# Hybrid SSD and attention layer on one core: weights times values in float32r high and low parts, head by head, row maxima a head ahead, one ring for the projection weights

## The chip, the cores and the metric

The kernel runs on one core of a Trainium2 chip. The metric is the device time of one execution in microseconds. The core's engines are TensorE (PE in the profile; PEld is its weight loading), VectorE (DVE), ScalarE (ACT), GpSimd (POOL) and SyncE (SP, which issues DMAs). Each runs its own queue of instructions in order.

## The reference

One layer is computed for 2048 new frames of one stream (the prompt) and for 16 frames of each of 8 streams (the sample), all in float32. An input projection is split between a state-space group (SSD) and an attention group of 8 heads of 64; both outputs go through one output projection; a gated feed-forward network with a short convolution follows (width 2816). The part that the change is about is the prompt's attention:

```python
def fox_block(q, k, v, fq, fk, q_pos, k_pos):
    s = jnp.einsum('bqhd,bkhd->bhqk', q, k).astype(jnp.float32) * FOX_SCALE
    s = s + (jnp.swapaxes(fq, 1, 2)[:, :, :, None] - jnp.swapaxes(fk, 1, 2)[:, :, None, :])
    s = jnp.where((k_pos[None, :] <= q_pos[:, None])[None, None], s, -jnp.inf)
    p = jax.nn.softmax(s, axis=-1)
    return jnp.einsum('bhqk,bkhd->bqhd', p.astype(v.dtype), v)
```

## The kernel before, in words

The prompt goes in four parts of 512 tokens (`p` = 0 to 3). For each, `a_head` norms and transposes the rows, the first step of `a_body` projects values, gates, queries and keys, and its second step projects the SSD inputs. Projections, the output projection and the feed-forward network multiply in float32r: both operands are split into a high and a low part (`split`: one engine copies the high part in float32r, another subtracts it to get the low part), and three matmuls are added up (high by high, high by low, low by high). Attention scores are made so too, with two matmuls (lines 576 and 577, or 635 and 636), as the parts are stacked on the 128 rows. The weights times values alone are plain float32 (line 621).

Projection weights come in two shapes. `proj_tm` keeps 128 tokens still and streams 256 or 272 weight columns; its split weights lie in `tmw`, one buffer for all eight row blocks. `proj_cm` keeps 128 weight columns still and streams the tokens; its split weights lie in `cmw`, two buffers, which also take the first input rows.

Attention for one part has two passes over a head's key blocks of 512 keys. `s_phase` makes scores with queries on the partitions, takes the row maximum of each block (line 580), the exponential with its sum (line 581), and, when the head is done, the final maximum and the reciprocal of the sum. These go through `st_d` in DRAM: the maximum comes back as two more rows of the query tile `q12`, the reciprocal into `rdb`. `t_phase` makes the scores again, with keys on the partitions and the maximum already subtracted, takes the exponential (line 640) and multiplies with the values (line 621) into the accumulator `pv`. It works on a pair of heads: for each step of 128 keys both heads' scores, then the weights times values of two steps before, each head on its own 64 columns of TensorE and its own half of `pv`. Line 649 scales by `rdb`. In part `p` there are 4(p+1) steps; the four of the diagonal block have 512, 384, 256 and 128 queries, the others 512.

`attention` runs `t_phase` of a pair with `s_phase` of the next pair strewn in, two steps to one, and with the steps of the SSD chunks (`ssd_chunk`) as side work. The order written in the program is a priority: a planner with its own costs decides the order on every engine, so that projections, output projection and attention mix. All DMAs but the weights' are issued from SP's queue; `dW` issues on ScalarE's.

Of the kernel before, what the change touches and what calls it, by code (L numbers as in the profile page):

```python
# [36 lines left out]
# windows of tokens: (first, end, with the sample's tokens behind them)  # L37
# [14 lines left out]
QB = 5  # L52
PB = 6
# [11 lines left out]
def hybrid_step(ctx: ExitStack, tc: tile.TileContext, i: dict, o: dict):  # L65
# [6 lines left out]
    # per head: queries (high; low) and (high; 1, 1, max high, max low), keys (high; high) and (low; F high, F low, 1, 1)  # L72
# [10 lines left out]
    st_d = dram.tile([H, 4, 3, 512], F32, name="st_d")  # L83
    sf_d = dram.tile([2, NB, H, PAST], F32, name="sf_d")
# [37 lines left out]
    # =================================================================== input projection  # L122
# [28 lines left out]
    def a_head(p, prev):  # L151
        res = []
        first = p == 0
        for e, w in enumerate(part_windows(p)):
# [12 lines left out]
            for c0, n, col, xsrc in groups:  # L167
                N = n * P
                pr = tpt()
                if first:  # L170
                    xa = at([P, 2, KT, P], "cmw", 2).rearrange("p c k d -> p c (k d)")
                    for c in range(n):
                        nc.scalar.dma_start(xa[:, c], i["xr"][c0 + c])
# [35 lines left out]
    def gates(p, dtf):  # L209
# [12 lines left out]
        # log(1 + u) = 2 atanh(u / (2 + u))  # L222
# [35 lines left out]
        # rows of the cumulated decays  # L258
# [9 lines left out]
        # rows of the negated cumulated log forget gates  # L268
# [15 lines left out]
        # the sample: decays of the states, cumulated log forget gates of its cached and new rows  # L284
# [39 lines left out]
    def a_body(p):  # L324
        """Two steps: queries, keys, values and gates; then the SSD inputs."""
        wins = wins_of[p]

        def proj_tm(src, n, use):
            wm = at([P, 2, KT, 272], "tmw", 1, F32R)
            for e in range(2):  # L330
                raw = at([P, 4, 272], "craw", 2)
                dW(raw[:, :, :n], src[:, 4 * e:4 * e + 4])
                split(raw[:, :, :n], wm[:, 0, 4 * e:4 * e + 4, :n], wm[:, 1, 4 * e:4 * e + 4, :n], S, G)
            for w, wt in wins:
                for c in win_tiles(w):
                    ps = mmt()
                    a = PAD1 + (c * P if c != SMP else w[1]) - w[0]
                    for k in range(KT):
                        T.matmul(ps[:, :n], wt[:, 0, k, a:a + P], wm[:, 0, k, :n], start=k == 0, stop=False)  # L339
                        T.matmul(ps[:, :n], wt[:, 0, k, a:a + P], wm[:, 1, k, :n], start=False, stop=False)  # L340
                        T.matmul(ps[:, :n], wt[:, 1, k, a:a + P], wm[:, 0, k, :n], start=False, stop=k == KT - 1)  # L341
                    use(ps, c)
# [108 lines left out]
    # =================================================================== SSD, one chunk of 128 tokens  # L451
# [94 lines left out]
    # =================================================================== prompt attention  # L546
# [67 lines left out]
    def t_phase(pair, qb, qq, rdb):  # L614
# [4 lines left out]
        def weigh(vr, jj, of, prs, first, last):  # L619
            for e in range(2):  # L620
                m = T.matmul(pv[e * 64:(e + 1) * 64, of:512], vr[:, jj, e * 64:(e + 1) * 64], prs[e][:, :512 - of],  # L621
                             start=first, stop=last)
                pv_ins.append(m.ins)

        for kb in order:
            kk = [load_k(2 * pair + e, kb) for e in range(2)]
            vr = load_v(pair, kb)
            for jj in range(4):
# [3 lines left out]
                prs = []  # L632
                for e in range(2):
                    ps = pss()
                    T.matmul(ps[:, :W], kk[e][:, 0, js], qq[e][:, 0, of:], start=True, stop=False)  # L635
                    T.matmul(ps[:, :W], kk[e][0:68, 1, js], qq[e][0:68, 1, of:], start=False, stop=kb != qb)  # L636
                    if kb == qb:
                        T.matmul(ps[:, 0:P], maskT, identb, start=False, stop=True)
                    pr = bt_([P, 528], "pr", PB)
                    S.activation(pr[:, :W], ps[:, :W], AF.Exp)  # L640
                    prs.append(pr)
                if len(late) == 2:
                    weigh(*late.pop(0))
                late.append((vr, jj, of, prs, kb == qb and jj == 0, kb == order[-1] and jj == 3))
# [3 lines left out]
        yl = bt_([P, 512], "yl", 2)  # L648
        V.tensor_mul(yl, pv, rdb)
        dS(mix_d[4 * qb:4 * qb + 4, :, 4 + pair, :].rearrange("c p t -> p c t"), yl.rearrange("p (c t) -> p c t", t=P))  # L650

    def attention(p, others):
        """All heads over the queries of part p, with the steps of other work strewn in; two steps of two pairs each."""
        def scores(pair, done):
            for e in range(2):
                yield from s_phase(2 * pair + e, p, done)

        cur = []
        for _ in scores(0, cur):
            pass  # L660
        for pair in range(4):
            if pair % 2 == 0:
                side = (None for g, _ in others[pair // 2] for _ in g)
                total = sum(n for _, n in others[pair // 2])
                units = 2 * 4 * (p + 1)
                k, given = 0, 0
            nxt = []
            ahead = scores(pair + 1, nxt) if pair < 3 else iter(())
            for _ in t_phase(pair, p, [c[0] for c in cur], cur[0][1]):
                next(ahead, None)  # L670
# [5 lines left out]
            for _ in ahead:  # L676
                pass
            cur = nxt
            if pair % 2:
# [4 lines left out]
    # =================================================================== sample attention  # L684
    def sample_attention():
# [6 lines left out]
        # eh[r, (h, t)] = r == h (rows 0..7 for the high parts, 32..39 for the low ones)  # L692
# [10 lines left out]
        # even and odd heads' rows  # L703
# [7 lines left out]
        # queries of a pair of heads (d of both; t of the one, t of the other)  # L711
# [6 lines left out]
        for b in range(NB):  # L718
# [53 lines left out]
            # ys[d, h, t, b]  # L772
# [4 lines left out]
    # =================================================================== output projection  # L777
# [41 lines left out]
    # =================================================================== FFN  # L819
# [3 lines left out]
    def prep(w, early=False):  # L823
        """The normed rows of a window, transposed and split; the rows themselves stay to be added to."""
# [92 lines left out]
    def ffn_part(x):  # L917
# [4 lines left out]
        for f0 in range(0, NFF, GRP):  # L922
# [10 lines left out]
            if f0 == 0 or f0 + GRP >= NFF:  # L933
                # window by window, so that the next window's rows can be made ready behind the first
# [3 lines left out]
                if f0 == 0 and x == 0:  # L938
                    # the rows to add to are not wanted before the first sums
# [23 lines left out]
    # =================================================================== order of the work  # L963
# [223 lines left out]
```

## Time and profile before

| | us |
|---|---|
| median of 3 runs | 3285.99 |
| lowest and highest run | 3285.44, 3288.5 |
| profiled execution, its span from first to last instruction | 3287.8 |
| TensorE busy in it | 3153.2 |
| VectorE, ScalarE, GpSimd busy in it | 1790.8, 1190.8, 835.9 |

The profiled execution has no time other than its span. The input projection, SSD and attention fill the first 1640 us; the feed-forward network, which the change leaves alone, takes the rest.

### The profile page before, as it was taken

How to read it: one execution, taken by the hardware profiler on the slowest of the kernel's cores; microseconds unless marked ns; L12 is line 12 of the kernel's file. 1: busy time of each engine (PE TensorE's matmuls, PEld its weight loads, DVE VectorE, ACT ScalarE, POOL GpSimd, SP SyncE). 2: the span in 40 equal slices, each digit the busy share in tenths (PEclk: the TensorE clock that was granted, in tenths of full speed). 3: DMA queues.
4: the chain of work that ended last, by engine and by line, in shares of the span. 5: the costliest groups of instructions: out<-in, count | busy, mean ns of one | idle time of the engine just before them, and what ended most of it. 6: DMA issues, size and time to landing. Idle time of an engine off the chain costs nothing.

```text
span 3287.8 us, 46925 instructions
## 1 busy us (share of the span) xinstructions
PE 3153.2 (96%) x18032; PEld 2662.5 (81%) x18032; DVE 1790.8 (54%) x3522; ACT 1190.8 (36%) x2378; POOL 835.9 (25%) x483
## 2 busy tenths in 40 slices
PE   5998989999999998999999999999999999999999
PEld 5876777668667775566689999998999999899998
DVE  5355446555554464334345555557555555766666
ACT  2343344445454455333332222224222223422222
POOL 3221221222131223000032232223222223333332
PEclk8989989999999998999999999999999999999999
DMA  4765875667456755555552122214212212322222
GB/s 148 212 192 178 266 207 175 179 187 211 138 174 171 211 152 178 155 157 158 173 172 64 58 65 64 65 55 138 64 53 76 64 52 71 110 78 75 71 73 70
DMA packets 227720, 423.96 MB, mean 129 GB/s; under 512 B 23264, under 2 KB 100072, under 8 KB 227496
## 3 DMA queue, kind: packets, MB, share of 16 engines
q1 hardware_dynamic: 173928, 259.72, 26.4%
q10 hardware_dynamic: 53568, 161.24, 16.1%
q8 instruction: 142, 2.33, 0.3%
q14 instruction: 82, 0.67, 0.1%
HBM read 342.43 MB, written 78.45 MB: 128 GB/s over the span
## 4 chain that ended last, share of the span: by engine, by line
PE 83%; DMA 10%; DVE 3%; SPq 1%; ACT 1%; issue 1%; POOL 0%; ACTq 0%; DVEq 0%; POOLq 0%
PE mm L112 13%; PE mm L113 13%; PE mm L114 13%; PE pv L621 6%; PE dn L901 5%; PE dn L902 5%; PE dn L903 5%; DMA k<-k_d 3%; PE dn L803 2%; PE dn L802 2%; PE dn L801 2%; PE s L635 2%; PE mm L339 2%; PE mm L340 2%; PE mm L341 2%; PE s L636 2%
## 5 line engine op out<-in xcount | busy, mean ns | idle before, releaser
L104 POOL TENSOR_TENSOR wr<-raw,wr 128x1024 fp32r<-128x1024 f32 x198 | 476.0, 2411 | 1038.7 <-ACT wr L101 1030.6
L112 PE MATMUL mm<-nT,wr 128*128 128x386 f32 (+1 forms) x2112 | 696.5, 330 | 1.5 <-ACT wr L101 1.0
L113 PE MATMUL mm<-nT,wr 128*128 128x386 f32 (+1 forms) x2112 | 695.3, 329 | 0.1
L114 PE MATMUL mm<-nT,wr 128*128 128x386 f32 (+1 forms) x2112 | 694.5, 329 | 0.2 <-POOL wr L104 0.2
L879 DVE SCALAR_TENSOR_TENSOR ac<-mm,cw,ac 128x384 f32<-128x384 f32 (+1 forms) x528 | 301.8, 572 | 345.7 <-ACT ac L877 338.0
L877 ACT ACTIVATE ac<-mm,cw 128x384 f32<-128x384 f32 (+1 forms) x264 | 172.5, 653 | 785.0 <-PE mm L114 777.0
L113 PEld LDWEIGHTS mm<-nT,wr 128*128 128x128 f32 x2112 | 399.4, 189 | 6.7 <-DVE nT L104 0.3
L112 PEld LDWEIGHTS mm<-nT,wr 128*128 128x128 f32 x2112 | 397.5, 188 | 8.1 <-ACT wr L101 1.5
L114 PEld LDWEIGHTS mm<-nT,wr 128*128 128x128 f32 x2112 | 398.0, 188 | 6.3 <-POOL wr L104 0.6
L904 DVE TENSOR_TENSOR y<-y,dn 128x512 f32<-128x512 f32 x374 | 255.2, 684 | 267.3 <-PE dn L903 264.6
L112 PE MATMUL mm<-nT,cmw 128*128 128x256 f32 (+2 forms) x1024 | 308.4, 301 | 14.0 <-ACT ev L395 7.9
L113 PE MATMUL mm<-nT,cmw 128*128 128x256 f32 (+2 forms) x1024 | 305.1, 298 | 0.0
L114 PE MATMUL mm<-nT,cmw 128*128 128x256 f32 (+2 forms) x1024 | 304.6, 297 | 0.0
L580 DVE TENSOR_REDUCE nm<-s 128x1 f32<-128x512 f32 (+2 forms) x320 | 189.8, 606 | 201.7 <-PE s L577 109.3
L901 PE MATMUL dn<-wr,ht 128*128 128x512 f32 x748 | 294.4, 394 | 2.8 <-DVE y L904 1.7
L902 PE MATMUL dn<-wr,ht 128*128 128x512 f32 x748 | 292.7, 391 | 0.0
L903 PE MATMUL dn<-wr,ht 128*128 128x512 f32 x748 | 290.1, 391 | 0.0
L101 ACT CAST wr<-raw 128x1024 fp32r<-128x1024 f32 x198 | 203.4, 1043 | 179.7 <-PE dn L903 161.5
L621 PE MATMUL pv<-pr,v 128*64 128x512 f32 (+3 forms) x640 | 265.1, 568 | 0.5 <-ACT pr L640 0.5
L104 POOL TENSOR_TENSOR cmw<-craw,cmw 128x1024 fp32r<-128x1024 f32 x64 | 154.1, 2409 | 433.0 <-ACT cmw L101 391.9
L581 ACT ACTIVATE s<-s,nm 128x512 f32<-128x512 f32 (+2 forms) x320 | 191.1, 598 | 172.9 <-DVE nm L580 158.4
L640 ACT ACTIVATE pr<-s 128x512 f32<-128x512 f32 (+3 forms) x320 | 163.0, 532 | 203.3 <-PE s L636 130.4
(295 smaller groups left out, 5474.2 us busy)
## 6 DMA issues: line engine op xcount, KB each, us to landing
raw<-in_w_up ACTq DMA_DIRECT2D x132, 512.0 KB
k<-k_d SPq DMA_DIRECT2D x160, 256.0 KB
raw<-in_w_down ACTq DMA_DIRECT2D x66, 512.0 KB
craw<-in_w_cm ACTq DMA_DIRECT2D x64, 512.0 KB
k<-k_d SPq DMA_DIRECT2D x160, 136.0 KB
craw<-in_w_tm ACTq DMA_DIRECT2D x24, 512.0 KB
q_d<-qk SPq DMA_DIRECT2D x96, 128.0 KB
k_d<-qk SPq DMA_DIRECT2D x96, 128.0 KB
```

Source lines behind the costliest of these rows:

```text
L101: S.copy(hi, src)
L104: leng.tensor_sub(lo, src, hi.bitcast(F32))
L112: T.matmul(ps[:, :W], whi(k), wt[:, 0, k, :W], start=k == 0, stop=False)
L113: T.matmul(ps[:, :W], whi(k), wt[:, 1, k, :W], start=False, stop=False)
L114: T.matmul(ps[:, :W], wlo(k), wt[:, 0, k, :W], start=False, stop=k == n - 1)
L581: S.activation(ps[:, :W], ps[:, :W], AF.Exp, bias=nm[:, qi, kb:kb + 1], accum_out=dn[:, qi, kb:kb + 1])
L621: m = T.matmul(pv[e * 64:(e + 1) * 64, of:512], vr[:, jj, e * 64:(e + 1) * 64], prs[e][:, :512 - of], start=first, stop=last)
L879: V.scalar_tensor_tensor(ac[:, 0:n], ps[:, j:j + n], cw2[:, ct, j:j + 1], ac[:, 0:n], op0=ALU.mult, op1=ALU.add)
L901: T.matmul(ps, ht[:, 0, ts_], wd[:, 0, cc], start=x == 0, stop=False)
L902: T.matmul(ps, ht[:, 0, ts_], wd[:, 1, cc], start=False, stop=False)
L903: T.matmul(ps, ht[:, 1, ts_], wd[:, 0, cc], start=False, stop=x == len(g) - 1)
L904: V.tensor_add(ys_[c][:, cc], ys_[c][:, cc], ps)
```

## The change

Comments are gone in the new file; else it is this:

- Values are kept a second time: each tile of projected values is split in high and low part (`vs`, one buffer) and written to `v2_d`, 128 columns a head (64 high, 64 low). `load_v` loads them for one head.
- `t_phase` takes one head. After the exponential, VectorE copies the high part of the weights in float32r and GpSimd subtracts it to get the low part (`pp`). Two float32r matmuls per step, high and low part of the weights, each with the 128 columns of high and low values, fill all of `pv`. At the end of a head ScalarE copies one half of `pv`, VectorE adds the other and multiplies by `rdb`.
- `attention` runs `s_phase` four steps (`LEAD`) further ahead, one step of it to one step of `t_phase`.
- `tmw` is gone: `proj_tm` takes two of three buffers of `cmw` (`WA`), one for each half of the row blocks.
- `q12` has 4 buffers instead of 5, `pr` 3 instead of 6. The buffer of norm2_g is moved to another pool.

```diff
-QB = 5
-PB = 6
+QB = 4
+PB = 3
+WA = 3
+LEAD = 4
...
+    v2_d = dram.tile([NTILE - 1, P, H, 2, HD], F32, name="v2_d")
...
-            wm = at([P, 2, KT, 272], "tmw", 1, F32R)
+            wm = []
             for e in range(2):
                 raw = at([P, 4, 272], "craw", 2)
                 dW(raw[:, :, :n], src[:, 4 * e:4 * e + 4])
-                split(raw[:, :, :n], wm[:, 0, 4 * e:4 * e + 4, :n], wm[:, 1, 4 * e:4 * e + 4, :n], S, G)
+                we = at([P, 2, 4, 272], "cmw", WA, F32R)
+                split(raw[:, :, :n], we[:, 0, :, :n], we[:, 1, :, :n], S, G)
+                wm.append(we)
...
                 dS(o["v"][c][:, half * 256:(half + 1) * 256], vt)
+                if c != SMP:
+                    vs = at([P, 4, 2, HD], "vs", 1, F32R)
+                    p4 = ps[:, 0:256].rearrange("p (h d) -> p h d", h=4)
+                    S.copy(vs[:, :, 0], p4)
+                    V.tensor_sub(vs[:, :, 1], p4, vs[:, :, 0].bitcast(F32))
+                    dS(v2_d[c][:, half * 4:half * 4 + 4], vs.bitcast(F32))
...
-            wc = at([P, 2, KT, P], "cmw", 2, F32R)
+            wc = at([P, 2, KT, P], "cmw", WA, F32R)
...
-    def load_v(pair, kb):
-        vr = bt_([P, 4, P], "v", 2)
-        dma(vr, o["v"][4 * kb:4 * kb + 4, :, pair * P:(pair + 1) * P].rearrange("c p d -> p c d"))
+    def load_v(h, kb):
+        vr = bt_([P, 4, P], "v", 2, F32R)
+        dma(vr.bitcast(F32), v2_d[4 * kb:4 * kb + 4, :, h].rearrange("c p a d -> p c (a d)"))
...
-    def t_phase(pair, qb, qq, rdb):
+    def t_phase(h, qb, q12, rdb, yl):
...
-        def weigh(vr, jj, of, prs, first, last):
-            for e in range(2):
-                m = T.matmul(pv[e * 64:(e + 1) * 64, of:512], vr[:, jj, e * 64:(e + 1) * 64], prs[e][:, :512 - of],
-                             start=first, stop=last)
+        def weigh(vr, jj, of, pp, first, last):
+
+            for a in range(2):
+                m = T.matmul(pv[:, of:512], vr[:, jj], pp[:, a, :512 - of], start=first and a == 0, stop=last and a == 1)
...
+                pr = bt_([P, 528], "pr", PB)
+                S.activation(pr[:, :W], ps[:, :W], AF.Exp)
+                pp = bt_([P, 2, 512], "pp", 3, F32R)
+                split(pr[:, :W], pp[:, 0, :W], pp[:, 1, :W], V, G)
+                late.append((vr, jj, of, pp, kb == qb and jj == 0, kb == order[-1] and jj == 3))
                 yield
         for x in late:
             weigh(*x)
-        yl = bt_([P, 512], "yl", 2)
-        V.tensor_mul(yl, pv, rdb)
...
+        e = h % 2
+        rs, ot = slice(e * 64, e * 64 + 64), slice(64 - e * 64, 128 - e * 64)
+        S.copy(yl[rs], pv[ot])
+        V.tensor_add(yl[rs], yl[rs], pv[rs])
+        V.tensor_mul(yl[rs], yl[rs], rdb[rs])
...
+        ahead = scores()
+        for h in range(H):
+            while len(done) <= h:
+                next(ahead, None)
+            if h == 0:
+                for _ in range(LEAD):
+                    next(ahead, None)
...
+            for _ in t_phase(h, p, *done[h], yl):
                 next(ahead, None)
                 k += 1
...
-    g2B = g2.tile([P, D], F32, name="g2B")
+    one = F.enter_context(tc.tile_pool(name="o3", bufs=1, side="right", reuse_waits="tile"))
+    g2B = one.tile([P, D], F32, name="g2B")
     dA(g2B, i["norm2_g"][0:1, :].to_broadcast([P, D]))
```

## Rows read from the trace of the kernel before

**Rows 1.** The page, its first two parts: busy time, share and instructions of TensorE (PE, and PEld for its weight loads), and the span in 40 equal slices of 82.2 us (tenths busy; PEclk is the granted TensorE clock in tenths of full speed).

```profile
PE 3153.2 (96%) x18032; PEld 2662.5 (81%) x18032; DVE 1790.8 (54%) x3522; ACT 1190.8 (36%) x2378; POOL 835.9 (25%) x483
PE   5998989999999998999999999999999999999999
PEclk8989989999999998999999999999999999999999
```

**Rows 2.** Busy time by stretch of the span, all engines. Columns: stretch, its length, then busy us (x instructions) of PE, PEld, DVE, ACT and POOL, granted clock, DMA share, GB/s.

```profile
0.00:390.00 390.00, 326.24 (x2311) 278.61 (x2311) 190.26 (x544) 135.88 (x321) 100.80 (x75) 0.92 0.64 194
390.00:1350.00 960.00, 903.27 (x5561) 668.10 (x5557) 501.45 (x1146) 466.03 (x1118) 222.96 (x128) 0.96 0.62 182
1350.00:1640.00 290.00, 290.00 (x1286) 187.69 (x1285) 111.25 (x210) 106.20 (x239) 10.08 (x18) 1.00 0.51 157
```

**Rows 3.** The same stretches for line 621 alone, the matmuls of weights times values. Columns: stretch, length, PE busy (x records), PEld busy, granted clock, DMA share, GB/s.

```profile
0.00:390.00 390.00, 20.56 (x64) 5.25 (x64) 0.92 0.64 194
390.00:1350.00 960.00, 178.60 (x416) 35.59 (x416) 0.96 0.62 182
1350.00:1640.00 290.00, 65.99 (x162) 13.05 (x160) 1.00 0.51 157
```

**Rows 4.** The timeline of TensorE at two places of the last part: start us, length us, engine, line, operation.

```profile
1477.02 0.39 PE L635 MATMUL s<-q,k 128*128 128x512 f32 x1
1477.02 0.19 PEld L636 LDWEIGHTS s<-q,k 68*128 68x128 f32 x1
1477.25 0.39 PE L636 MATMUL s<-q,k 68*128 68x512 f32 x1
1477.57 1.07 PE L621 MATMUL pv<-pr,v 128*64 128x512 f32 x2
1478.57 0.50 PE L802 MATMUL dn<-wo,mx 128*128 128x512 f32 x1
1478.91 0.39 PE L803 MATMUL dn<-wo,mx 128*128 128x512 f32 x1
...
1499.55 0.39 PE L636 MATMUL s<-q,k 68*128 68x512 f32 x1
1499.87 1.08 PE L621 MATMUL pv<-pr,v 128*64 128x512 f32 x4
1500.88 0.50 PE L801 MATMUL dn<-wo,mx 128*128 128x512 f32 x1
```

**Rows 5.** The first and the last stretch of line 621 in the timeline of TensorE. In between the 640 records of the line stand in 264 stretches with other instructions between them.

```profile
156.87 1.07 PE L621 MATMUL pv<-pr,v 128*64 128x512 f32 x2
...
1621.88 2.79 PE L621 MATMUL pv<-pr,v 128*64 128x512 f32 x10
```

**Rows 6.** Groups of TensorE's instructions by line and shape: count, busy us, mean ns of one, idle time before them and what ended it.

```profile
L621 PE MATMUL pv<-pr,v 128*64 128x512 f32 x448 | 219.3, 636 | 0.5 <-ACT pr L640 0.5
L339 PE MATMUL mm<-tmw,nT 128*128 128x256 f32 x408 | 121.7, 301 | 4.1 <-ACT tmw L101 2.3 <-ACT ev L349 1.8
L636 PE MATMUL s<-q,k 68*128 68x512 f32 x224 | 92.9, 415 | 11.9 <-DMA q<-st_d 9.5 <-DMA k<-k_d 2.3
```

**Rows 7.** Groups on the other engines, same columns: the nearest operations to those that are added.

```profile
L104 POOL TENSOR_TENSOR nT<-qk,nT 128x512 fp32r<-128x512 f32 x1 | 1.3, 1295 | 5.3 <-ACT nT L101 5.3
L104 POOL TENSOR_TENSOR cmw<-craw,cmw 128x1024 fp32r<-128x1024 f32 x64 | 154.1, 2409 | 433.0 <-ACT cmw L101 391.9 <-PE mm L112 11.8 <-DMA xb_d<-cth 7.7
L103 DVE CAST ht<-ac 128x384 fp32r<-128x384 f32 x110 | 39.3, 357 | 2.9
L103 DVE CAST ht<-ac 128x256 fp32r<-128x256 f32 x22 | 6.3, 287 | 0.4
L649 DVE TENSOR_TENSOR yl<-pv,rdb 128x512 f32<-128x512 f32 x16 | 11.0, 689 | 37.5 <-PE pv L621 30.4 <-DMA out_s_ssdT<-yl 5.7 <-DMA k_d<-qk 1.4
L392 DVE SCALAR_TENSOR_TENSOR qk<-mm,qk 128x256 fp32r<-128x256 f32 x64 | 27.0, 423 | 115.8 <-ACT qk L391 94.0 <-DMA k<-k_d 7.9 <-DMA q_d<-qk 5.4
```

**Rows 8.** One VectorE operation by shape (groups by line), and the timeline of POOL and VectorE where two of their operations meet.

```profile
L890 DVE TENSOR_TENSOR ac<-ac 128x384 f32<-128x384 f32 x110 | 173.5, 1577 | 3.7
L890 DVE TENSOR_TENSOR ac<-ac 128x256 f32<-128x256 f32 x22 | 11.3, 514 | 1.2
...
20.91 2.36 POOL L104 TENSOR_TENSOR nT<-qk,nT 128x1024 fp32r<-128x1024 f32 x1
20.95 2.34 DVE L1001 TENSOR_SCALAR abc<-abc 128x8 f32<-128x8 f32 x1
```

**Rows 9.** The timeline of ScalarE in the first 60 us: the last read of the second tile of input rows, the first cast of projection weights, and two copies of value tiles.

```profile
17.10 0.19 ACT L183 ACTIVATION_READ_ACCUMULATOR cmw<-cmw 128x1 f32 x1
17.29 1.08 ACT L101 CAST tmw<-craw 128x1088 fp32r<-128x1088 f32 x1
...
45.37 0.37 ACT L349 COPY ev<-mm 128x256 f32<-128x256 f32 x1 [1.18 <-PE mm L341]
48.43 0.37 ACT L349 COPY ev<-mm 128x256 f32<-128x256 f32 x1 [2.16 <-issue]
```

**Rows 10.** Two pieces of the chain that ended last (start us, us, what: a DMA from issue to landing, of 128 KB), and the load of the values in the list of DMA issues (count, KB each).

```profile
91.30 2.23 DMA q_d<-qk
387.77 7.43 DMA q_d<-qk
...
v<-out_v SPq DMA_DIRECT2D x40, 256.0 KB
```

More of the change, by code (lines that the diff above doesn't have):

```diff
@@ L617, in t_phase @@
         late = []
-        def weigh(vr, jj, of, prs, first, last):
-            for e in range(2):
-                m = T.matmul(pv[e * 64:(e + 1) * 64, of:512], vr[:, jj, e * 64:(e + 1) * 64], prs[e][:, :512 - of],
-                             start=first, stop=last)
+        def weigh(vr, jj, of, pp, first, last):
+            for a in range(2):
+                m = T.matmul(pv[:, of:512], vr[:, jj], pp[:, a, :512 - of], start=first and a == 0, stop=last and a == 1)
                 pv_ins.append(m.ins)
         for kb in order:
-            kk = [load_k(2 * pair + e, kb) for e in range(2)]
-            vr = load_v(pair, kb)
+            kk = load_k(h, kb)
+            vr = load_v(h, kb)
             for jj in range(4):
@@ L631, in t_phase @@
                 js = slice(jj * P, (jj + 1) * P)
[L632 to L641, printed above, removed]
+                ps = pss()
+                T.matmul(ps[:, :W], kk[:, 0, js], q12[:, 0, of:], start=True, stop=False)
+                T.matmul(ps[:, :W], kk[0:68, 1, js], q12[0:68, 1, of:], start=False, stop=kb != qb)
+                if kb == qb:
+                    T.matmul(ps[:, 0:P], maskT, identb, start=False, stop=True)
                 if len(late) == 2:
                     weigh(*late.pop(0))
-                late.append((vr, jj, of, prs, kb == qb and jj == 0, kb == order[-1] and jj == 3))
+                pr = bt_([P, 528], "pr", PB)
[3 more added lines that the diff above has]
+                late.append((vr, jj, of, pp, kb == qb and jj == 0, kb == order[-1] and jj == 3))
                 yield
@@ L647, in t_phase, with scores @@
             weigh(*x)
-        yl = bt_([P, 512], "yl", 2)
-        V.tensor_mul(yl, pv, rdb)
-        dS(mix_d[4 * qb:4 * qb + 4, :, 4 + pair, :].rearrange("c p t -> p c t"), yl.rearrange("p (c t) -> p c t", t=P))
-    def attention(p, others):
[L654 to L665, printed above, removed]
+        e = h % 2
[3 more added lines that the diff above has]
+        V.tensor_mul(yl[rs], yl[rs], rdb[rs])
+        if e:
+            dS(mix_d[4 * qb:4 * qb + 4, :, 4 + h // 2, :].rearrange("c p t -> p c t"), yl.rearrange("p (c t) -> p c t", t=P))
+    def attention(p, others):
+        done = []
+        def scores():
+            for h in range(H):
+                yield from s_phase(h, p, done)
+        ahead = scores()
+        for h in range(H):
+            while len(done) <= h:
[3 more added lines that the diff above has]
+                    next(ahead, None)
+            if h % 4 == 0:
+                side = (None for g, _ in others[h // 4] for _ in g)
+                total = sum(n for _, n in others[h // 4])
+                units = 4 * 4 * (p + 1)
                 k, given = 0, 0
[L667 to L670, printed above, removed]
+            if h % 2 == 0:
+                yl = bt_([P, 512], "yl", 2)
+            for _ in t_phase(h, p, *done[h], yl):
                 next(ahead, None)
@@ L675, in attention @@
                     given += 1
[L676 to L679, printed above, removed]
+            if h % 4 == 3:
                 for _ in side:
@@ L1057, in hybrid_step @@
     tp = F.enter_context(tc.tile_pool(name="t3", bufs=2, reuse_waits="tile"))
-    g2 = F.enter_context(tc.tile_pool(name="g2", bufs=1, reuse_waits="tile"))
     O = ExitStack()
@@ L1065, in hybrid_step @@
     B.close()
-    g2B = g2.tile([P, D], F32, name="g2B")
+    one = F.enter_context(tc.tile_pool(name="o3", bufs=1, side="right", reuse_waits="tile"))
+    g2B = one.tile([P, D], F32, name="g2B")
     dA(g2B, i["norm2_g"][0:1, :].to_broadcast([P, D]))
-    one = F.enter_context(tc.tile_pool(name="o3", bufs=1, side="right", reuse_waits="tile"))
     yp = F.enter_context(tc.tile_pool(name="y3", bufs=YB, side="right", reuse_waits="tile"))
```

9 lines of the change are left out of this document (5 added, 4 removed).

## Prediction

> **What bounds the kernel now.** I read the page first. TensorE is busy for 96% of the span, and its slices show 9 nearly everywhere after the first half of the attention; the digit of the granted clock falls to 8 only in four of the first 16 slices [rows 1]. So time is TensorE's work plus its idle time plus what runs at half clock. The table by stretch splits the first 1640 us, the only ones that the change touches [rows 2]. From 0 to 390 us (part 0, the sample, the first projections) TensorE idles for 64 us of 390 at clock 0.92: chains between engines set the pace. From 390 to 1350 us it idles for 57 of 960, clock 0.96. From 1350 to 1640 us it never idles, at full clock, with VectorE at 111 and GpSimd at 10 us. I call these A, B and C. The same table for line 621 alone shows what the change attacks: 20.6, 178.6 and 66.0 us, 265 in all [rows 3]. 0.2% (6.6 us) is about what a measurement of this kernel can tell from no change; I use it as the bound below.
>
> **Weights times values on TensorE.** 320 head-steps (a head, 128 keys) are made, 224 of them with 512 queries (448 records in [rows 6], two a matmul) and 96 narrower. The timeline shows one float32 head-step at full width: it starts at 1477.57 and the next instruction at 1478.57, 1.00 us; two heads standing side by side take 1.01 together (1499.87 to 1500.88), since they use different columns [rows 4]. But the planner mostly separates them: 264 stretches for 320 head-steps [rows 5]. Around a stretch there is more: line 636 gives way after 0.32 us instead of 0.23, and the first float32r matmul behind gives way after 0.34 instead of 0.23. That is 0.20 us a stretch, of which 0.07 already counts in the busy time (1.07 drawn, 1.00 to the next start). So 265 + 264 x 0.13 = 299 us: A 24, B 199, C 76.
>
> After, a head-step is two float32r matmuls. At 512 columns such a matmul gives way after 0.23 us [rows 4], so 0.47. For the narrow ones the weight load of 0.19 us is the floor [rows 4]: 0.38. A has 8 wide and 24 narrow head-steps, C about 65 and 15, B the other 151 and 57. At the clocks of [rows 2] that is 12.9 / 0.92 = 14 us in A, 92.6 / 0.96 = 96 in B, 36 in C. TensorE is relieved of 10, 103 and 40 us, 153 in all.
>
> **What is added on the other engines.** Each head-step gets a subtraction on GpSimd: 1.30 us at 512 columns, and by the line through that and 2.41 at 1024 [rows 7], 1.02, 0.74 and 0.46 for the narrow ones: 224 x 1.30 + 32 x 2.22 = 362 us, of which B gets 57 x 0.74 + 151 x 1.30 = 238. It also gets a cast on VectorE, nearest the casts of 357 ns at 384 and 287 at 256 [rows 7], so 0.43 at 512 and 0.22 at 128: 81 us in B. At the end of a head come an add and a multiply on VectorE where a pair had one multiply of 0.69 [rows 7]; half the partitions, the same columns, so I take 0.69 each: 2.1 us more a pair, 20 in B. Each of 32 value tiles gets a copy of 0.37 on ScalarE [rows 9] and a subtraction like the 0.42 of line 392 [rows 7], 10 us of VectorE in B.
>
> These two engines don't run freely beside each other. A multiply on VectorE takes 514 ns at 256 columns and 1577 at 384, and a tiny operation that should take a fraction of a us lasts from 20.95 to 23.29 while a GpSimd subtraction runs from 20.91 to 23.27 [rows 8]: VectorE waits until GpSimd is through. The Trainium skill says why ("SBUF — State Buffer", Who interferes with whom): a VectorE copy or cast in its two-port mode, or an operation with two SBUF inputs, and a GpSimd operation lock each other out for a whole instruction; the trace agrees, 2.34 us beside 2.36. By that rule cast and subtraction cannot overlap, so no step would be shorter than 0.43 + 1.30 = 1.73 us, which by itself would bind nowhere here, but would load VectorE as in the second rival.
>
> In B GpSimd goes from 223 to 461 of 960 us, 48%. A cast that starts meanwhile waits half of a 1.30 or 2.41 us operation, weighted 0.92 us, so 0.44 us on average: 92 us for 208 casts (zero if the planner keeps them apart, 270 if each waits for a whole 1.30). VectorE in B: 501 + 81 + 92 + 20 + 10 = 704 us, of 857 if all of TensorE's relief were kept: 82%, against 52% now. Behind a late cast stand the row maxima (line 580) for the next head; for them waits ScalarE's exponential (line 581), and that frees the four score banks that TensorE writes next. Behind a late subtraction stand the splits of projection weights. TensorE has two steps between scores and weights times values, and a step takes 4.6 us in B (960 / 208), so the new chain of exponential, cast and subtraction mostly fits, and TensorE has other matmuls meanwhile. At 82% with strict order, part of the relief becomes idle time: between all and nothing I take half in B, 52 us. In C VectorE goes from 111 to some 180 of 250 us and GpSimd from 10 to 107: room enough, I keep 40 less 3 for the longer end of each head, 37. There the cover is the output projection's matmuls; without them the last heads would wait 1.7 us a step.
>
> In A the 10 us stand against two losses. `vs` has one buffer: a value tile now takes 0.37 + 0.42 and a DMA, 2.23 us at best and 7.43 at worst for half the bytes [rows 10], so 3.0 to 8.2 us, where copies follow each other after 3.06 us now [rows 9]. With nothing else for TensorE to do at the start, eight tiles may lose 0 to 40 us; the first few hide under the copies of rows still being normed, I take 8. The chain of a step is 1.73 us longer in a part with four steps a head: 8 heads, about half of it uncovered, 7 us. A gives back 5 us.
>
> **Edits that cost nothing or little.** The shared weight ring is free at the start: the second tile of input rows is last read at 17.10, the first weight cast starts at 17.29 [rows 9]. Later a half can be split before the previous projection ends; line 339 idles for 4.1 us at 256 columns. Row maxima a head ahead remove waits for the maximum's way through DRAM, 9.5 us before line 636 [rows 6]. Of these 13.6 us I count 8 (0 to 13.6). Key loads keep their number; with one head per step four buffers reach twice as far ahead. Value loads double, 40 to 80 of 256 KB [rows 10], and 32 writes of 256 KB come: 19 MB and 72 issues more on SP's queue, behind which the key loads stand; the DMA share is 0.62 in B and 0.51 in C [rows 2], so I take nothing and put a few us into the range. Fewer `pr` and `q12` buffers match one head at a time: nothing. The norm2_g buffer is loaded later; its cover is the output projection at the seam, and without that it costs one landing, up to 7.43 us.
>
> **Sum.** B 52 + C 37 - A 5 + 8 = 92 us less. The profiled span of 3287.8 becomes 3195.8; the median of the runs stands 1.8 us below the span, so 3194.
>
> **Rivals.** *All is kept* (15%): the planner hides the longer chain entirely, TensorE stays as full as now; 153 and the 13.6 us of idle time go: 3286 - 167 = 3119. For it speaks that TensorE waits for the exponential for only 0.5 us in 448 wide records [rows 6]; against it, that B already idles for 57 us with VectorE at 52%.
>
> *VectorE becomes the bound in B* (17%): if the waits for GpSimd come at a whole operation, 270 instead of 92 us, VectorE reaches 882 of 857 us. B then keeps nothing; with C at 30 and A at -10, 20 us remain: 3266. The long multiply in [rows 8] speaks for it, where a multiply of 384 columns takes three times one of 256 on average; against it, that row maxima read PSUM and need not wait.
>
> *Slower: TensorE's queue waits for the low part* (10%). Its order is fixed by a planner. If that counts on a shorter subtraction than 1.30 us, or on a GpSimd that isn't in a weight split of 2.41, each head-step's second matmul holds up all that stands behind it. It decides from 153 / 320 = 0.48 us a head-step on; at 0.6 us (half of a split's 2.41 us, met half of the time) the loss is 192 - 153 = 39 us: 3325, before any half-clock time. For it: the 0.5 us of idle time before line 621 [rows 6] come from a chain of one engine, and now three stand in a row. Against it: the two steps of slack.
>
> **How the numbers follow.** The forecast gets 58%; its own range, with 20 to 80% of B kept, is 3225 to 3163. 8 in 10 need most of the VectorE rival too and reach almost to full keeping: 3122 to 3275; outside lie the slower rival, and the better half of the full one. Faster by over 0.2%: 58 + 15 + most of 17, 0.87. Within 0.2%: the thin stretch between the VectorE rival and the slower one, 0.03. Slower: 0.10.
>
> **What would show it.** In the profile after: the new line of weights times values with 640 float32r matmuls, starts 0.23 us apart, some 150 us of TensorE; no 1.00 us holes. GpSimd's subtractions about 360 us, casts of 0.43 us alone and up to 1.7 beside a subtraction; VectorE's busy time up by 150 to 300 us. The seam to the feed-forward network at about 1550 instead of 1640 us, most of it won between 390 and 1350. The step on B is wrong if TensorE's idle time there grows by far more or less than 50 us; the forecast is wrong if TensorE waits before the new matmuls for GpSimd by more than 0.3 us a step, or if the start (up to 120 us) is over 20 us later because of the value tiles.

## The result, and the profile after

The changed kernel takes 3242.17 us (median; 3236.41 to 3244.7) where the kernel before took 3285.72 beside it: a ratio of 0.987, with an interval of 0.9855 to 0.9888. That is 44 us less; 92 were forecast. The profiled execution has a span of 3241.4 us. All of the difference lies ahead of the feed-forward network: its first up-projection matmul starts at 1639.2 us instead of 1684.5, and from there on both kernels take 1.60 ms.

The first part of the page after, as in [rows 1]:

```profile
PE 3038.1 (94%) x18032; PEld 2741.7 (85%) x18032; DVE 2049.0 (63%) x3922; ACT 1216.5 (38%) x2442; POOL 1229.2 (38%) x803
PE   5988889799989997999899999999999999999999
PEclk9999989899989998998999999999999999999999
```

The three stretches of [rows 2] for all engines, and then for the new line 635 alone, as line 621 in [rows 3]:

```profile
0.00:390.00 390.00, 322.97 (x2460) 289.38 (x2461) 220.46 (x626) 152.66 (x363) 140.46 (x110) 0.95 0.70 221
390.00:1350.00 960.00, 854.00 (x5598) 746.24 (x5596) 685.10 (x1398) 482.48 (x1152) 488.33 (x346) 0.93 0.65 196
1350.00:1640.00 290.00, 272.80 (x1310) 214.84 (x1310) 178.57 (x313) 114.40 (x260) 105.07 (x98) 0.95 0.53 176
...
0.00:390.00 390.00, 19.20 (x64) 11.80 (x64) 0.95 0.70 221
390.00:1350.00 960.00, 157.94 (x434) 82.16 (x434) 0.93 0.65 196
1350.00:1640.00 290.00, 54.24 (x142) 28.14 (x142) 0.95 0.53 176
```

From 390 to 1350 us TensorE idles for 106 us instead of 57. The last stretch, full and at full clock before, has 17 us of idle time and a granted clock of 0.95, so a tenth of it runs at 1.2 GHz instead of 2.4.

The groups that answer to [rows 6, 7 and 9]:

```profile
L635 PE MATMUL pv<-pp,v 128*128 128x512 f32 x448 | 181.9, 441 | 35.1 <-DVE yl L663 17.4 <-POOL pp L108 13.1 <-DVE pp L107 3.9
L647 PE MATMUL s<-q,k 68*128 68x512 f32 x224 | 93.2, 416 | 5.3 <-DMA k<-k_d 3.2 <-DMA q<-st_d 2.1
L108 POOL TENSOR_TENSOR pp<-pr,pp 128x512 fp32r<-128x512 f32 x224 | 305.0, 1366 | 352.9 <-DVE pp L107 331.8 <-ACT ev L356 6.7 <-DVE mh L108 5.0
L107 DVE CAST pp<-pr 128x512 fp32r<-128x512 f32 x224 | 137.6, 619 | 48.2 <-ACT pr L653 44.1 <-PE pv L635 3.0
L663 DVE TENSOR_TENSOR yl<-yl,pv 64x512 f32<-64x512 f32 x32 | 21.8, 682 | 12.0 <-ACT yl L662 11.6
L664 DVE TENSOR_TENSOR yl<-yl,rdb 64x512 f32<-64x512 f32 x32 | 27.4, 857 | 0.6
L361 ACT CAST vs<-mm 128x256 fp32r<-128x256 f32 x32 | 12.0, 374 | 35.8 <-DMA v_d<-vs 34.8 <-DVE bs L485 1.0
```

Line 635 waits 35.1 us at full width, where line 621 waited 0.5. The timeline at the end of a head in the last part, TensorE first, then GpSimd, then VectorE at the same time:

```profile
1532.17 0.68 PE L635 MATMUL pv<-pp,v 128*128 128x512 f32 x2
1533.71 0.78 PE L635 MATMUL pv<-pp,v 128*128 128x512 f32 x2 [0.85 <-POOL pp L108]
1535.53 0.74 PE L635 MATMUL pv<-pp,v 128*128 128x512 f32 x2 [1.04 <-POOL pp L108]
...
1532.38 1.28 POOL L108 TENSOR_TENSOR pp<-pr,pp 128x512 fp32r<-128x512 f32 x1 [0.36 <-DVE pp L107]
1534.02 2.70 POOL L108 TENSOR_TENSOR pp<-pr,pp 128x512 fp32r<-128x512 f32 x2 [0.37 <-DVE M L600]
...
1532.22 0.68 DVE L593 TENSOR_REDUCE nm<-s 128x1 f32<-128x512 f32 x1
1532.82 1.12 DVE L107 CAST pp<-pr 128x512 fp32r<-128x512 f32 x1
1534.28 1.23 DVE L107 CAST mh<-M 128x4 fp32r<-128x4 f32 x1
1535.54 1.20 DVE L108 TENSOR_TENSOR mh<-M,mh 128x4 fp32r<-128x4 f32 x1
```

TensorE moves at the pace of GpSimd's subtractions here, two of them in 2.70 us. And VectorE's two operations on 128x4 elements last 1.2 us each, nearly as long as a subtraction of 1.35, and end where the two subtractions end.

### The profile page after: what moved, and what is told of

It reads as the page before. It is cut to its first block, busy times and chain, and to the rows that moved or that the text cites. A ratio compares the mean times of both kernels' runs of the same rounds, so it can differ in the third digit from the quotient of the medians.

```text
span 3241.4 us, 48271 instructions
## 1 busy us (share of the span) xinstructions
PE 3038.1 (94%) x18032; PEld 2741.7 (85%) x18032; DVE 2049.0 (63%) x3922; ACT 1216.5 (38%) x2442; POOL 1229.2 (38%) x803
## 4 chain that ended last, share of the span: by engine, by line
PE 70%; DMA 13%; DVE 10%; issue 3%; ACT 2%; POOL 2%; SPq 1%; ACTq 0%; DVEq 0%; POOLq 0%
PE mm L116 13%; PE mm L117 12%; PE mm L118 12%; PE dn L919 5%; PE dn L920 5%; PE dn L921 5%; PE pv L635 2%; DMA sg<-ac_d 2%; DVE pp L107 1%; PE dn L819 1%; PE dn L820 1%; PE dn L821 1%; DMA k<-k_d 1%; PE s L646 1%; PE s L589 1%
## 5 line engine op out<-in xcount | busy, mean ns | idle before, releaser
L108 POOL TENSOR_TENSOR pp<-pr,pp 128x512 fp32r<-128x512 f32 (+1 forms) x320 | 384.9, 1207 | 469.6 <-DVE pp L107 439.5
L108 POOL TENSOR_TENSOR cmw<-craw,cmw 128x1024 fp32r<-128x1024 f32 (+1 forms) x96 | 234.6, 2446 | 256.1 <-ACT cmw L105 237.9
L635 PE MATMUL pv<-pp,v 128*128 128x512 f32 (+3 forms) x640 | 231.4, 405 | 50.0 <-DVE yl L663 17.4
L653 ACT ACTIVATE pr<-s 128x512 f32<-128x512 f32 (+1 forms) x320 | 167.8, 532 | 182.3 <-PE s L647 118.4
```

Of the source, the lines that this page charges most:

```text
L108: leng.tensor_sub(lo, src, hi.bitcast(F32))
L635: m = T.matmul(pv[:, of:512], vr[:, jj], pp[:, a, :512 - of], start=first and a == 0, stop=last and a == 1)
```

## The account that the experiments share

For each kernel the table by stretch is taken from the start to the first up-projection matmul: length, then busy us of PE, PEld, DVE, ACT and POOL, granted clock. Length less PE is TensorE's idle time. In order: before; after; high half alone, two multiplications; before with float32r; after with the copy on ScalarE; high half alone, one multiplication; float32 at full width.

```profile
0.00:1684.50 1684.50, 1564.01 (x9364) 1171.44 (x9365) 825.91 (x1934) 723.20 (x1710) 338.30 (x234) 0.96 0.61 182
0.00:1639.20 1639.20, 1449.29 (x9365) 1250.30 (x9366) 1083.33 (x2334) 748.89 (x1774) 733.06 (x554) 0.94 0.64 198
0.00:1583.60 1583.60, 1419.27 (x9364) 1244.34 (x9365) 856.92 (x2014) 746.09 (x1774) 342.93 (x234) 0.95 0.66 205
0.00:1577.80 1577.80, 1378.85 (x9044) 1199.83 (x9045) 822.47 (x1934) 736.03 (x1750) 339.14 (x233) 0.94 0.63 194
0.00:1611.80 1611.80, 1438.10 (x9365) 1246.03 (x9366) 923.51 (x2013) 894.50 (x2094) 717.26 (x554) 0.95 0.65 202
0.00:1544.20 1544.20, 1363.57 (x9045) 1190.38 (x9045) 853.82 (x2013) 745.88 (x1774) 341.69 (x234) 0.94 0.67 210
0.00:1629.80 1629.80, 1502.74 (x9365) 1233.34 (x9365) 851.36 (x2013) 753.45 (x1774) 340.77 (x234) 0.97 0.65 199
```

Before to after: TensorE's busy time fell by 115 us, and its idle time rose from 120 to 190, so 45 us were won. The profile's granted clock stands at half (1.2 GHz instead of 2.4) for 140 us before and for 198 after. If half of TensorE's busy time in it counts as lost, that is 60 and 77 us, so 17 us of the relief went to the clock.

Two theories stand from here. **The added chain takes it**: cast and subtraction, on two engines that block each other, cost what is missing. **The relief itself is worth less**: TensorE's matmuls cover the other engines' chains, so of what they give up only a part comes off the end. Times below are medians, with the ratio to the kernel before measured beside each.

## Experiments

**High half alone.** ScalarE's exponential goes to the high half, no copy, no subtraction, both multiplications take that half (it counts double; the low part of the weights is left out):

```
-m = T.matmul(pv[:, of:512], vr[:, jj], pp[:, a, :512 - of], ...)
+m = T.matmul(pv[:, of:512], vr[:, jj], pp[:, 0, :512 - of], ...)
...
-pr = bt_([P, 528], "pr", PB)
-S.activation(pr[:, :W], ps[:, :W], AF.Exp)
+S.activation(pp[:, 0, :W], ps[:, :W], AF.Exp)
-split(pr[:, :W], pp[:, 0, :W], pp[:, 1, :W], V, G)
```

> The changed kernel, with ScalarE's exponential written straight into the high half in float32r; VectorE's copy of the high part and GpSimd's subtraction are gone, and TensorE multiplies the high half twice. The low part of the weights is left out of the result; TensorE's work is the same as in the changed kernel. Theory (the engines behind the split weights eat the gain: 198 us of VectorE, 385 us of GpSimd, and TensorE's waits for the two halves, 47.0 us in 60 waits for the low and 36.2 us in 37 for the high): 50 to 80 us come back, 3162 to 3192 us, and TensorE's idle time up to the first up-projection falls from 193 us towards the 127 us of the kernel before. Rival (TensorE's own work was mis-sized and the waits only move to the next late instruction): under 20 us come back, 3222 us or more.

3186.57 us, 0.971 (0.969 to 0.973): 55 us come back, inside the first theory's range. Third row of the account: TensorE is busy for 30 us less (13 of them because 154 us instead of 198 are at half clock) and idle for 26 us less. But it is 93 us below the kernel before, where the prediction's sum without these two operations would give about 150. Both theories are needed.

**The kernel before, in float32r.** Weights and values are rounded, no low parts (left out), one matmul of 128 columns for a head and step (both heads' values go into the same sums, which this kernel does not tell apart):

```
-QB = 5
+QB = 4
...
+v2 = bt_([P, 4, P], "v2", 2, F32R)
+S.copy(v2, vr)
...
-m = T.matmul(pv[e * 64:(e + 1) * 64, of:512], vr[:, jj, e * 64:(e + 1) * 64], prs[e][:, :512 - of], ...)
+m = T.matmul(pv[:, of:512], vr[:, jj], prs[e][:, :512 - of], ...)
...
-pr = bt_([P, 528], "pr", PB)
+pr = bt_([P, 528], "pr", PB, F32R)
```

> The kernel before, pairs of heads as they were, but weights and values rounded to float32r with no low parts (both are left out of the result), one matmul for a head and step with all 128 columns of the pair; ScalarE rounds each of the 40 value tiles (about 0.6 us each, 24 us in all, a guess from its 128x512 copies), and there are 4 query buffers in place of 5. No copy of high parts and no subtraction. The weighing should take about 320 x 0.23 less the narrow ones = 70 us in place of 244. Theory A (all of 0.20 us for each float32 stretch belonged to the change of type): TensorE's work up to the first up-projection falls by 174 + 53 = 227 us, 3059 to 3085 us with the waits unchanged. Theory B (half of that extra stands around any matmul that waits on a semaphore): it falls by about 200 us, 3086 to 3110 us. Theory C (what TensorE gives up turns into waiting for ScalarE and VectorE in the middle stretch): over 3130 us, with TensorE idle over 180 us in place of 127.

3187.55 us, 0.972 (0.969 to 0.975): theory C. TensorE is busy for 185 us less (fourth row), and nothing was added but 40 copies on ScalarE (with one query buffer less); its idle time still rose from 120 to 199 us. Hardly any of it stands before the weighing:

```profile
L623 PE MATMUL pv<-pr,v 128*128 128x512 f32 x224 | 99.6, 459 | 2.6 <-ACT pr L641 2.6
```

It is spread over the waits that were there before: score banks held by ScalarE, key loads, the row maxima's way through DRAM (17.5 instead of 9.5 us).

**The copy of the high part on ScalarE.**

```
-split(pr[:, :W], pp[:, 0, :W], pp[:, 1, :W], V, G)
+split(pr[:, :W], pp[:, 0, :W], pp[:, 1, :W], S, G)
```

> The changed kernel, with the copy of the high part made by ScalarE right behind its exponential instead of by VectorE; nothing else moves. Takes about 198 us from VectorE's 1083 us ahead of the up-projections and adds about 165 us (320 copies at some 0.5 us) to ScalarE's 749. Theory (VectorE's queue holds the high part up, and VectorE and GpSimd hold each other up): 15 to 40 us faster than the changed kernel, 3202 to 3227 us, and the waits on VectorE's copy, 36.2 us, go. Rival (ScalarE becomes the engine that is late, since the next exponential stands behind the copy): 3242 to 3275 us.

3216.16 us, 0.980 (0.977 to 0.983), and on another chip:

> The kernel with the high part copied by ScalarE once more, beside the two built on it and on the same chip: its ratio to the kernel before was 0.980 (0.977 to 0.983), and the kernel with the carried head ends had 0.984 on another chip. If the carried ends are really slower, this one comes out again at 0.979 to 0.982; if chip and run make the difference, at 0.983 or more.

3210.15 us, 0.9775 (0.975 to 0.980). So 26 to 32 us of the 55 are the copy's place: VectorE goes from 1083 to 924 us, ScalarE from 749 to 895 (fifth row), and ScalarE's queue has the room. It is faster than both kernels given, with the same computation.

**The low part on VectorE too** (the same line with `S, V`):

> The changed kernel with the high part copied by ScalarE and the low part subtracted by VectorE; GpSimd has no part in the weights. VectorE then does 320 subtractions at about 0.65 us where the changed kernel has it do 320 copies at 0.62 us, so its total stays at about 1090 us ahead of the up-projections; GpSimd loses 385 us. Theory (it is the length of the chain, most of it GpSimd's 1.37 us for a subtraction, that TensorE waits for): faster than the kernel with only the copy moved (3216 us), 3190 to 3210 us. Rival (VectorE's load is what makes all other work late): 3225 to 3245 us, as the changed kernel.

3233.95 us, 0.9855 (0.984 to 0.987): no different from the changed kernel and slower than with GpSimd's subtraction, although VectorE's takes 777 ns where GpSimd's takes 1335. The shorter chain did not pay for 223 us on VectorE's queue. Between these two kernels VectorE's load mattered more than the chain's length.

**The accumulator freed without VectorE.**

```
-S.copy(yl[rs], pv[ot])
-V.tensor_add(yl[rs], yl[rs], pv[rs])
+y2 = bt_([P, 512], "y2", 1)
+S.copy(y2[rs], pv[ot])
+S.copy(yl[rs], pv[rs])
+V.tensor_add(yl[rs], yl[rs], y2[rs])
```

> The changed kernel, with ScalarE copying both halves of the accumulator out of PSUM, and VectorE adding them from SBUF, so that the one accumulator is free without VectorE. Theory (the single accumulator, emptied 32 times through VectorE's queue, costs the 32.3 us in 14 waits that stand on VectorE's addition): 10 to 25 us faster than the changed kernel, 3217 to 3232 us. Rival (those waits cover others that stand right behind): 3235 to 3245 us.

3241.66 us, 0.987 (0.985 to 0.990): nothing. The wait named in the profile did go, from 17.4 to 2.5 us, and the line's own from 35.1 to 16.0:

```profile
L635 PE MATMUL pv<-pp,v 128*128 128x512 f32 x448 | 178.5, 434 | 16.0 <-POOL pp L108 9.1 <-DVE pp L107 4.1 <-ACT yl L664 2.5
```

TensorE's whole idle time stayed at 189 us; other waits took the place.

**Head ends carried into the next head.** `late` lives on from head to head (emptied only at heads 3 and 7), and the accumulator is emptied behind its last weighing:

```
...
-        for x in late:
-            weigh(*x)
+        if h % 4 == 3:
+            while late:
+                weigh(*late.pop(0))
```

> The kernel with the high part copied by ScalarE, and in it the last two weighings of a head put behind the first score matmuls of the next head instead of straight behind the last exponential, except at every fourth head; the accumulator is emptied there too. In the changed kernel 22.3 us of TensorE's waits, in 21 places, stand between two weighings at a head's end; with the copy on ScalarE 9.7 us in 17 places. Theory (a head's end has nothing to cover the chain, and there are 32 of them where the kernel before had 16): 6 to 15 us faster than with the copy on ScalarE alone (3216 us), 3201 to 3210 us. Rival (the waits come back a few matmuls later, on the one accumulator): 3212 to 3222 us.

3230.90 us, 0.984 (0.982 to 0.985): 0.4 and 0.6% slower than the two measurements of its base, of which the first one's interval still touches it. Waits between two weighings remained (11 us in 14 places, 7 to 10 in the base). A miss for the theory; why it is slower rather than the same stays open.

**No lead.** `LEAD = 0`:

> The changed kernel with LEAD = 0: the score steps of the next head no longer start four steps early, everything else as it is. Theory (the lead is worth the 9.5 us that the kernel before waits in seven places for the row maxima's round trip through DRAM, and no more): 4 to 12 us slower than the changed kernel, 3246 to 3254 us. Rival (the lead costs as much at each part's start as it brings): 3238 to 3246 us.

3270.91 us, 0.997 (0.996 to 0.998): about 30 us slower, outside both theories. What was to be removed is back, larger than before the change:

```profile
L647 PE MATMUL s<-q,k 68*128 68x512 f32 x224 | 95.8, 427 | 28.7 <-DMA q<-st_d 28.5
```

Our reading: head by head, a next head's maxima have half the time to come back from DRAM that a next pair's had. With the four steps of lead the line waits for 5.3 us.

**More lead.** `LEAD = 8`, with the copy on ScalarE:

> The kernel with the high part copied by ScalarE, and the score steps of the next heads eight steps ahead in place of four. Without a lead the changed kernel took 29 us more, 28.6 us of TensorE's waits standing on the row maxima's way through DRAM. Theory (the more lead the fewer waits): 5 to 15 us faster than the same kernel with a lead of four, 3201 to 3211 us by its first comparison, 3216 us. Rival (four steps have done it already): within 5 us of it.

3235.96 us, 0.986 (0.984 to 0.988), 26 us slower than a lead of four on the same chip. Line 647 waits for nothing, but with a lead of four and the copy on ScalarE it waited for only 0.1 us. TensorE's idle time rose from 170 to 203 us, and the waits for the last VectorE operation on a finished head's sums (line 608) from 11 to 45 us. The transposes of finished heads are among them, with eight steps and with four (the copy on ScalarE, second measurement):

```profile
L613 PE MATMUL s<-ident,rd 128*12 128x128 f32 x32 | 9.6, 299 | 21.7 <-DVE rd L608 21.7
...
L613 PE MATMUL s<-ident,rd 128*12 128x128 f32 x32 | 9.3, 290 | 11.6 <-DVE rd L608 10.8 <-DVE rd L611 0.8
```

**Two buffers for the split values** (`"vs", 2`, with the copy on ScalarE):

> The kernel with the high part copied by ScalarE, and two buffers in place of one for the split values on their way to DRAM. In the changed kernel ScalarE waits 34.8 us for that one buffer. Theory (the wait makes the kernel's start late): 3 to 8 us faster than with one buffer. Rival (other waits of TensorE stand behind it at once): within 3 us of it.

3215.50 us, 0.979 (0.976 to 0.982), against 0.9775 with one: the rival. ScalarE's wait for that buffer fell from 40.6 to 1.9 us, and nothing hung on it. Three buffers were meant for the changed kernel itself, but their pool needs 110.8 KB a partition where 110.5 are left, so that kernel was not measured.

**One multiplication.** The high half alone, `for a in range(1)`; the low part of the weights is left out:

> The kernel with the high half alone (no copy, no subtraction), with one multiplication for a step where it has two: 320 matmuls of the weighing are left out, some 74 us of TensorE's time at 147.6 us for 640; every other engine does the same work. The result leaves the low part of the weights out. Theory (TensorE's own time sets the pace): all of it comes off, 3186.6 - 74 = 3110 to 3120 us. Rival (the matmuls of the weighing cover the other engines' chains, so that what TensorE gives up comes back as waits and as time at the half clock): 20 to 60 % of it comes off, 3142 to 3172 us, with TensorE's idle time ahead of the up-projections up by 25 us or more over 166 us.

3151.11 us, 0.959 (0.957 to 0.962). Of the 74 us reckoned only 35 came off, 47%: the rival. The line itself gave 64 us (147.6 to 83.4 from start to start without idle time; the second matmul of a pair is the cheaper one); the other lines took some 9 us more, and 16 us became idle time (sixth row). So 35 us came off for 56 us less of busy TensorE, 64%. This is the fastest kernel of the study, with weights in float32r without their low part.

**The same, in float32.** The exponential is written in float32, and the matmul reads both operands as float32:

```
-m = T.matmul(pv[:, of:512], vr[:, jj], pp[:, 0, :512 - of], ...)
+m = T.matmul(pv[:, of:512], vr[:, jj].bitcast(F32), pp[:, :512 - of], ...)
-pp = bt_([P, 2, 512], "pp", 3, F32R)
-S.activation(pp[:, 0, :W], ps[:, :W], AF.Exp)
+pp = bt_([P, 512], "pp", 3)
+S.activation(pp[:, :W], ps[:, :W], AF.Exp)
```

> The kernel with one multiplication for a step (3151 us), and in it only the type changed: ScalarE writes the exponential in float32, and TensorE multiplies it in float32 with the same 128 columns (the value tiles still come through float32r, and the high half of the weights is now all of the weights). All other engines, the order and the buffers stay. 320 float32 matmuls of 1.00, 0.78, 0.58 and 0.36 us by the kernel before are some 279 us where 83 stood, 196 more. Theory A (the prediction's: each change of type costs 0.20 us beside, and TensorE's time counts in full): 196 + 64 = 260 us more, 3390 to 3420 us. Theory B (the type alone costs next to nothing beside, TensorE's time counts in full): 3335 to 3365 us. Theory C (in this stretch TensorE's time counts about half, as when the second multiplication was left out, 35 of 74 us): 3240 to 3290 us, with TensorE idle for 40 us or more less than the 181 us of the kernel with one multiplication.

3236.45 us, 0.985 (0.983 to 0.987): below every theory's range, with TensorE idle for 54 us less, as theory C had it. The float32 matmul was cheaper than the kernel before had it. A step at full width, the next matmul, and the one after that:

```profile
908.16 1.08 PE L635 MATMUL pv<-pp,v 128*128 128x512 f32 x2
908.67 0.68 PE L346 MATMUL mm<-cmw,nT 128*128 128x256 f32 x1
909.19 0.28 PE L347 MATMUL mm<-cmw,nT 128*128 128x256 f32 x1
```

It gives way after 0.51 us, and the next matmul after 0.52 instead of its usual 0.12: 0.91 us for the step. By the medians of 195 such steps it is 0.46 and 0.40, and nothing ahead, where 64 columns took 1.00, with 0.09 more ahead and 0.11 behind. TensorE's busy time is 139 us above the float32r kernel's, the time 85: 61%.

This run also says how little of the change's gain needs float32r. It has the full width, the order head by head, the lead and the ring, but float32 weights, no cast and no subtraction, and it leaves nothing out. It takes what the changed kernel takes; their intervals overlap. How that gain divides between the width, the order, the lead and the ring was not measured. From here, float32r with two multiplications is worth 50 us (to 3186.57), and cast and subtraction cost 55.

## Why the prediction was only half right

The direction held, and the time lies inside the range of 3122 to 3275, but outside the likeliest case's own, 3163 to 3225.

- **Losses: right as a sum.** The prediction gave 61 us back (51 in B, 3 in C, 15 in A, less 8 for the edits); TensorE's idle time rose by 69. In B the step held: 49 us more [rows 2, and the table after]. The rest is partly luck: by the same tables A idles for 3 us more and C for 17. The threshold of 0.3 us of waiting for GpSimd a step was never near: 16.4 us before line 635 in all, 0.05 a step. Cast and subtraction cost 55 us by the run without them.
- **The step that failed: 153 us of relief for TensorE**, measured 115. Counted from start to start without idle time, the line went from 247 to 162 us: 85, where the prediction had 100 (246 to 146). The other lines got 30 us shorter, where the 0.20 us around each of 264 stretches should have given 53. What the sum had no term for is a change of the clock: with busy time at half clock counted as half, the line went from 237 to 148 and the other lines from 1267 to 1224, 131 us of relief, and the clock took 17 of it. The rest, 22 us, is in the sizes. One that shows: a float32r matmul of line 635 that starts after idle time gives way after 0.34 us, not 0.23 (21 of 21 at full width).
- **The 0.20 us around a float32 stretch was read rightly.** Against matmuls of the same shape elsewhere, those ahead of a stretch took 0.09 us more and those behind it 0.11 (medians of 264; 55 us together). Around line 635 both medians are 0 (9 us together). Ahead of float32 on 128 columns there is nothing either, so the 0.09 is not the type's alone.
- **The same failure by place: the relief of C, kept in full because TensorE never idled there.** For C the prediction kept 37 of 40. By the first matmul of the output projection 52 us were won (1332.6 to 1280.2), close to the 55 for A, B and the edits; at the seam 45. So C won little or nothing: it lost 7 by this count, with some 10 us more of attention's work left in it. From that matmul to the seam, before and after; then 80 us of the last heads in the changed kernel, and the like stretch without cast and subtraction:

```profile
1332.60:1684.50 351.90, 351.90 (x1600) 236.51 (x1600) 143.60 (x266) 126.49 (x284) 15.58 (x32) 1.00 0.53 166
1280.20:1639.20 359.00, 342.06 (x1655) 270.78 (x1655) 220.11 (x390) 143.46 (x329) 130.70 (x120) 0.96 0.55 182
...
1500.00:1580.00 80.00, 65.53 (x293) 45.98 (x292) 56.47 (x91) 32.35 (x73) 45.66 (x39) 0.81 0.39 123
1440.00:1520.00 80.00, 78.11 (x415) 62.74 (x414) 34.30 (x66) 36.69 (x81) 3.85 (x6) 0.98 0.53 168
```

  "Room enough" was true of busy time. But the prediction itself named the output projection as the cover, and the last heads have little of it left: 27 of its matmuls from 1500 to 1580 us, 105 in the last 80 us of weighing before, 132 in the run without cast and subtraction. There TensorE ran at GpSimd's pace, idled, and lost its clock: C has 17 us of idle time and, by half of the busy time in 31 us at half clock, 13 us of lost work, 30 where 3 were reckoned. Without cast and subtraction these are 5 and 4 us; as the planner's order differs too, how much of that is the order's was not separated.
- **TensorE's relief is not worth its length.** Two runs put a price on a microsecond of TensorE's busy time: 64 and 61% of it.
- **Lead and ring: 8 us, too small for the lead.** It is worth about 30 here, but against head by head without one, a loss that the prediction did not see either. The ring was not tried by itself; the freed space is needed by the rest.
- **VectorE as the bound**: half right. Its busy time rose by 257 us, inside 150 to 300, the casts took 198 us (0.62 each, where 0.43 and a wait of 0.44 were forecast), and taking them off it gave 26 to 32 us back. It reached 71% in B, not the 100% at which the rival would decide; the moved copy shows that its load costs time well below that.
- **Value tiles**: the second to fifth of the projections' copies were 4 to 5 us later, where 8 were reckoned, and that cost nothing that two buffers could bring back.

The Trainium skill ("SBUF — State Buffer", Who interferes with whom) says that a VectorE copy or cast in its two-port mode, or an operation with two SBUF inputs, and a GpSimd operation that reads SBUF lock each other out, and that a reduction doesn't take part. The timeline above agrees: a cast and a difference on 128x4 elements at 1.2 us beside subtractions, a row maximum at 0.68 beside one that began at 1532.38.

What stays open: why carried head ends and a lead of eight are slower by 15 to 26 us, beyond the named waits; and whether the clock in C would have held without the idle time, since they come together. The planner makes a new order for every kernel: the first matmul of the output projection comes at 1210 to 1299 us in the kernels after the change, at 1220 and 1257 in two that take the same time. Part of any difference between two kernels may be the order, and no run separates it.

## What to carry to other kernels

Time taken off the busiest engine counts in full only while it covers nothing: measure the exchange by leaving some of its work out (56 us less of busy TensorE gave 35) before paying for relief with work on other engines. Before a change of type, try the old type in the new shape; here float32 at full width, in the new order, had the whole gain. A wait that the profile names can vanish without any gain, so judge an edit by the engine's whole idle time.

## What was not expected of the hardware

- Two operations of VectorE on 128x4 elements took 1.23 and 1.20 us beside GpSimd's subtractions. A multiply of 64x512 from SBUF took 857 ns on average, an addition of that size that reads PSUM 682.
- A float32 matmul of 512 columns took 0.86 us (median) with what it held up when it used 128 columns of the array, and 1.20 with 64.
- Behind a bf16 or plain float32 matmul, the first float32r matmul of a score step (line 646, 512 columns, full clock) gave way after 0.30 us or more in all 58 cases of the changed kernel; behind another float32r matmul, without idle time before it, in 7 of 143, with a median of 0.23.
- Kernels with more idle time mostly had more time at half clock: 120 us of idle time and 140 at half clock before, 190 and 198 after, 199 and 198 in the kernel before with float32r, 127 and 102 at full-width float32. But not in step: 203 and 181 with a lead of eight.
